# Modulation weights of layer 1 in half blocks, with two f32 tiles and one step per up iteration, in a two-layer diffusion block on Trainium2

## The chip, the cores and the metric

The kernel runs on one core of a Trainium2 chip. The metric is the device time of one execution in microseconds, here the median of three runs. Five engines work side by side and wait for each other by semaphores: TensorE (PE in the profile, its weight loads PEld), VectorE (DVE), ScalarE (ACT), GpSimd (POOL) and SyncE (SP), which issues the loads from HBM.

## The reference, cut to what matters

The reference is a model of two transformer-like layers with a conditioning vector, followed by a second block of four branches. The change touches the conditioning of layer 1 and runs during the feed-forward part (FFN) of layer 0. Shapes: 256 context tokens and 256 latent tokens, width 1024, FFN width 2816.

```python
D_MODEL = 1024
SEQ = 256
CTX_LEN = 256
D_FF = 2816

def modulate(x, g, shift, scale):
    return rmsnorm(x, g) * (1 + scale) + shift

def conv_ffn(h, w_up, conv_w, conv_b, w_down, rows):
    u = h @ w_up
    if rows is None:
        u = dwconv1d(u, conv_w[1], conv_b)
    else:
        u = dwconv2d_grid(u, conv_w, conv_b, rows)
    a, g = jnp.split(u, 2, axis=-1)
    return (jax.nn.silu(g) * a) @ w_down
```

In each layer six vectors of 1024 (shift, scale and gate for the mixer and for the FFN) are computed for the latent and for the context stream: a 1024-vector of the condition times a matrix `mod_w[layer]` of 1024 x 6144 in float32, plus `mod_b`. For layer 1 these are 24 MB of weights for two vectors, and they are needed when layer 1 begins (the first two), and later (the others).

## The kernel before

Weights come as float32 blocks of 1 MB. `get_w` (L318) loads a block into an f32 tile `st` by SyncE (`load_w`, L313), makes the high part `whi` in float16 on ScalarE (L324) and the low part `wlo` = `st` - `whi` in bfloat16 on VectorE or, with `eng=self.G`, on GpSimd (L325). The f32 tile is free again when the low part is done; the parts are free when TensorE has used them. Every product is three passes: high weights with high and low activations, low weights with high activations (`proj_fm`, L328).

`mod_steps` (L487) is a generator: one call of `next` runs one step. For one of the six vectors (`r`) it goes through four blocks `b` of 128 x 2048, that is two chunks of 128 rows by 1024 columns. A step loads and splits a block and multiplies it on TensorE: sixteen matmuls of 256 columns into one PSUM tile `mod`, four at a time in four column groups of the array. After the fourth block the row is copied out and turned into columns by small matmuls (L508).

`ffn(0, BOTH)` (L966) computes layer 0's FFN for all 512 tokens. *Up*: 22 iterations, each with one 1 MB block of `w_up`, split with GpSimd; two tiles of 24 matmuls with 512 columns; a 3x3 or 3-tap convolution on VectorE; the gating on ScalarE and GpSimd; the split of the result into `hid`. The first three iterations have their context half done ahead. *Down*: eight output tiles `k`, each from two half tiles of `w_dn` (128 x 1408, 704 KB), split with VectorE; 33 matmuls a half tile. For `k` = 0 to 5 a matmul has 512 columns. Tiles 6 and 7 are done for the context stream first (256 columns), then come its norm for layer 1, and then the same tiles for the latent stream. `layer1_mixer` begins with the products `dt` and `sx` on the normed context tokens.

The modulation steps of layer 1 are pulled in between: in up after every second iteration and after iteration 10 (twelve steps), in down after every half tile (twelve more). All their low parts are made on GpSimd. Their pools are `ms`, one f32 tile of 128 x 2048, and `mp`, two of each part.

The program is written in this order, and a planner with its own cost model orders the instructions on each engine before the run: at each point it takes the first instruction of the program that is ready by its costs. On the chip each engine, and SyncE's queue of loads, works through its list in that fixed order and waits where something is not there yet. With `start` and `stop` matmuls of one PSUM tile may stand apart, so the lists mix down and modulation matmuls.

Of the kernel before, what the change touches and what calls it, by code (L numbers as in the profile page):

```python
# [236 lines left out]
def bc(ap, axis, n):  # L237
    a = ap.unsqueeze(axis)
    shp = list(a.shape)
    shp[axis] = n  # L240
    return a.to_broadcast(shp)
# [7 lines left out]
class Program:  # L249
# [234 lines left out]
            self.stt(modA[:, 0, :, 2 * b:2 * b + 2], modc[:, r, :, 2 * b:2 * b + 2], 1.0, bc(g, 1, 2),  # L484
                     ALU.add, ALU.mult)

    def mod_steps(self, l, r, tag="mm", eng=None, pool=None, parts=None, whole=False):  # L487


        T, modc = self.T, self.modc[l]  # L490
        ps = self.ps(tag, "mod")
        for b in range(4):
            src = self.I["mod_w"][6 * l + r - 2, b]
            if whole:
                terms = [(self.cs, self.load_w(src, 2048, pool).rearrange("p (k n) -> p k n", k=2))]
            else:
                terms = [(self.c3, w) for w in self.get_w(src, 2, 1024, eng, pool, parts)]
            for k in range(2):
                for i, (c, w) in enumerate(terms):
                    for j in range(4):  # L500
                        T.matmul(ps[32 * j:32 * j + 32, :256], c[:, 2 * b + k], w[:, k, 256 * j:256 * j + 256],
                                 start=b == k == i == 0, stop=b == 3 and k == 1 and i == len(terms) - 1)
            if b < 3:
                yield
        row = self.cols.tile([128, 256], F32, tag="mrow", name="mrow", bufs=1)
        self.act(row, ps[:, :256])
        for c in range(2):
            T.matmul(ps[:, 256 + 8 * c:264 + 8 * c], row[:, c * 128:c * 128 + 128], self.msel8, start=True, stop=True)  # L508
        self.tt(modc[:, r].rearrange("p s (j c) -> p s j c", c=2), ps[:, 256:272].rearrange("p (c j s) -> p s j c", c=2, j=4),
                bc(self.modb[:, l, r].rearrange("p (j c) -> p j c", c=2), 1, 2), ALU.add)  # L510
        if r in (1, 4):
            self.stt(self.modA[l][:, r // 4], modc[:, r], 1.0, bc(self.ng[r // 4][:, l], 1, 2), ALU.add, ALU.mult)
        yield
# [452 lines left out]
    def ffn(self, l, streams):  # L966
        I, V = self.I, self.V
        both = len(streams) == 2
        n, t0 = (512, 0) if both else (256, 256)
        lat = n - 256  # L970
        fcb = self.pp("fcb").rearrange("p (l c) -> p l c", l=2)[:, l]
        h = self.h
        if both:

            self.norm_stream(l, 1, 1)
            first = []
            for i in range(3):
                w = self.get_w(I["w_up"][l, i], 8, 256, self.G)
                first.append((w, [self.mm("up") for _ in range(2)]))
                for c in range(2):  # L980
                    self.proj_fm(first[i][1][c][:, :256], w, c * 128, 128, h, 0, 256)
        else:
            self.norm_h(self.xT, t0, n, self.segs(l, 1, streams), h)

        def conv(u, ps, c):
            w = lambda j: fcw[:, c, j:j + 1]
            self.act(u[:, :n], ps[:, :n], AF.Identity, bias=fcb[:, c:c + 1], scale=w(4))
            if both:
                self.stt(u[:, 1:256], ps[:, 0:255], w(3), u[:, 1:256], ALU.mult, ALU.add)
                self.stt(u[:, 0:255], ps[:, 1:256], w(5), u[:, 0:255], ALU.mult, ALU.add)  # L990
            ug, pg = [a[:, lat:lat + 256].rearrange("p (r c) -> p r c", r=4) for a in (u, ps)]
            for dy in (-1, 0, 1):
                for dx in (-1, 0, 1):
                    if dy == 0 and dx == 0:
                        continue
                    r0, r1, c0, c1 = max(0, -dy), 4 - max(0, dy), max(0, -dx), 64 - max(0, dx)
                    o = ug[:, r0:r1, c0:c1]
                    self.stt(o, pg[:, r0 + dy:r1 + dy, c0 + dx:c1 + dx], w(3 * dy + dx + 4), o, ALU.mult, ALU.add)

        with ExitStack() as ph:  # L1000
            fp = self.pool("fp", 1, None, ph)
            f2 = self.pool("f2", 3, None, ph)
            stage = self.pool("stage", 1 if both else 3, None, ph)
            fcw = fp.tile([128, 44, 9], F32, name="fcw")
            self.nc.sync.dma_start(fcw, I["fcw"][l].rearrange("p (c j) -> p c j", c=44))
            hid = self.pair(fp, "hid", [128, 22, n])
            if both:
                ms, mp = self.pool("ms", 1, None, ph), self.pool("mp", 2, None, ph)
                mods = chain.from_iterable(self.mod_steps(1, r, eng=self.G, pool=ms, parts=mp) for r in range(6))
            for i in range(22):  # L1010
                begun = both and i < 3
                if begun:
                    w, pss = first[i]
                else:
                    w = self.get_w(I["w_up"][l, i], 8, 256, self.G, (None, stage)[i % 2])
                us = []
                for c in range(2):
                    ps = pss[c] if begun else self.mm("up")
                    a = 256 if begun else 0
                    self.proj_fm(ps[:, a:n], w, c * 128, 128, h, a, n)  # L1020
                    u = f2.tile([128, n], F32, tag=f"u{c}", name="u")
                    conv(u, ps, 22 * c + i)
                    us.append(u)
                sg = f2.tile([128, n], F32, tag="sg", name="sg")
                self.act(sg[:, :n], us[1][:, :n], AF.Silu)
                self.tt(sg[:, :n], sg[:, :n], us[0][:, :n], ALU.mult, eng=self.G)
                self.split(hid[0][:, i], hid[1][:, i], sg[:, :n], eng=self.G)
                if both and (i % 2 or i == 10):
                    next(mods)

            def down(k, ws, a, b):
                ps = self.mm("dn")
                for j, w in enumerate(ws):
                    self.proj_fm(ps[:, a:b], w, 0, 128, hid, a, b, nk=11, h0=11 * j, first=j == 0, last=j == 1)
                    if both:
                        next(mods, None)
                return ps

            def weights(k, j, parts=None):
                return self.get_w(I["w_dn"][l, 2 * k + j], 11, 128, self.G if not both and k < 2 else None, (None, stage)[j], parts)  # L1040

            if not both:
                self.ahead()
            for k in range(6 if both else 8):
                self.add_residual(down(k, [weights(k, j) for j in range(2)], 0, n), l, 5, k, streams, t0)
                if not both:
                    self.before_norm(k)
                    if k >= 4 and k < 4 + 3:
                        for i in (0, 1):
                            self.first_mg.append(self.get_w(I["w2_m"][2 * (k - 4) + i], 8, 128, self.G, stage, self.nx, 2048, 1024))  # L1050
            if both:

                ws = [[weights(k, j, fp if (k, j) == (7, 1) else None) for j in range(2)] for k in (6, 7)]
                for s, a, b in streams:
                    for k in (6, 7):
                        ps = down(k, ws[k - 6], a, b)
                        self.add_residual(ps[:, a:b], l, 5, k, ((s, 0, 256),), a)
                    if s == 0:
                        self.norm_stream(1, 0, 0)
# [878 lines left out]
```

## Time and profile before

| what | us |
|---|---|
| median of 3 runs (lowest, highest) | 1708.39 (1706.92, 1712.79) |
| the profiled execution, its time | 1712.42 |
| its span in the profile | 1710.6 |
| TensorE busy | 1601.9 (94%) |
| VectorE busy | 1198.7 (70%) |
| ScalarE busy | 845.7 (49%) |
| GpSimd busy | 538.7 (31%) |
| loads of `mod_w`, whole kernel | 40 of 1 MB |
| mean granted TensorE clock | 0.954 |

The profile is one execution. All times of the trace are counted from the start of the span; 1.8 us of the profiled execution lie around it. Busy shares are means over stages with different limits. A matmul's end is modelled, so a busy TensorE can also be one that waits between matmuls; the number of matmuls in a stretch tells more. Layer 0's FFN spans about 370 to 757 us: up until 610, down behind it.

### The profile page before, as it was taken

The page shows a single profiled execution, that of the slowest core. Times are in us where ns is not written, and L with a number is a line of the kernel's source. Part 1 is how long each engine was busy: PE and PEld are TensorE (multiplying, and loading weights), DVE is VectorE, ACT ScalarE, POOL GpSimd, SP SyncE. Part 2 cuts the span into 40 slices and gives each one's busy share as a digit, 9 for nine tenths or more (in the row PEclk, how much of TensorE's full clock was granted, in tenths as well). Part 3 has the DMA queues.
Part 4 walks back from the last instruction along what each step waited for, and adds up shares of the span by engine and source line. Part 5 has one row for each costly group of instructions (what it writes and reads, how often), then busy time and mean ns, then how long its engine had stood idle before and what let it go on. Part 6 is the DMA issues. An engine that isn't in the chain of part 4 may idle for free.

```text
span 1710.6 us, 31683 instructions
## 1 busy us (share of the span) xinstructions
PE 1601.9 (94%) x12978; PEld 1103.3 (64%) x12978; DVE 1198.7 (70%) x2600; ACT 845.7 (49%) x1366; POOL 538.7 (31%) x277
## 2 busy tenths in 40 slices
PE   6999999889999999898989898779999999999998
PEld 3566865476444444475566666568887787777877
DVE  5888745788778864457777676889976885455834
ACT  4746524445555443335554545356664644556442
POOL 0000000226887742311100000059954412332150
PEclk8999999899999999989989898989999989989999
DMA  9222127723443334432213222255455343333551
GB/s 380 95 86 75 52 86 260 298 102 127 145 172 133 128 139 172 153 121 88 86 50 123 73 100 80 76 195 198 153 183 201 112 161 124 118 142 105 222 173 50
DMA packets 37731, 236.78 MB, mean 138 GB/s; under 512 B 4304, under 2 KB 5072, under 8 KB 14672
## 3 DMA queue, kind: packets, MB, share of 16 engines
q1 hardware_dynamic: 37584, 234.74, 38.7%
q8 instruction: 102, 1.67, 0.4%
q14 instruction: 45, 0.37, 0.1%
HBM read 233.68 MB, written 1.05 MB: 137 GB/s over the span
## 4 chain that ended last, share of the span: by engine, by line
PE 74%; DVE 12%; ACT 4%; DMA 4%; issue 3%; POOL 2%; ACTq 0%; SPq 0%; DVEq 0%; POOLq 0%
PE up L332 19%; PE sx L332 5%; PE fm L332 4%; PE mg L332 4%; DVE wlo L294 3%; PE dn L332 3%; ACT whi L306 2%; PE sz L332 2%; PE br L332 2%; PE tm L339 2%; PE so L332 2%; DMA st<-in_mod_w_dram 2%; PE eo L332 2%; PE mqk L332 2%; PE sc L1601 2%
## 5 line engine op out<-in xcount | busy, mean ns | idle before, releaser
L294 POOL TENSOR_TENSOR wlo<-st,whi 128x2048 bf16<-128x2048 f32 (+2 forms) x114 | 408.1, 3584 | 923.7 <-ACT whi L306 873.6
L332 PEld LDWEIGHTS <-whi 128*128 128x128 f16 (+3 forms) x5240 | 517.3, 100 | 265.0 <-issue 40.6
L306 ACT ACTIVATE whi<-st 128x2048 f16<-128x2048 f32 (+3 forms) x218 | 365.5, 1685 | 318.4 <-DMA st<-in_mod_w_dram 59.1
L332 PEld LDWEIGHTS <-wlo 128*128 128x128 bf16 (+1 forms) x2620 | 261.2, 100 | 128.0 <-issue 11.8
L303 DVE SCALAR_TENSOR_TENSOR u<-up,fcw,u 128x189 f32<-128x189 f32 (+3 forms) x792 | 298.7, 433 | 47.9 <-ACT u L306 38.7
L294 DVE TENSOR_TENSOR wlo<-st,whi 128x2048 bf16<-128x2048 f32 (+3 forms) x104 | 242.0, 2330 | 108.5 <-ACT whi L306 107.3
L332 PE MATMUL up<-hh,whi 128*128 128x256 f16 (+1 forms) x752 | 239.4, 320 | 2.7 <-ACT hh L306 1.8
L332 PE MATMUL up<-hl,whi 128*128 128x256 bf16 (+1 forms) x752 | 239.1, 320 | 2.7 <-DVE hl L303 2.7
L332 PE MATMUL up<-hh,wlo 128*128 128x256 f16 (+1 forms) x752 | 238.6, 319 | 0.0
L332 PE MATMUL dn<-hidh,wlo 128*128 128x256 f16 (+1 forms) x396 | 124.0, 315 | 2.0 <-DVE wlo L294 2.0
L332 PE MATMUL dn<-hidh,whi 128*128 128x256 f16 (+1 forms) x396 | 124.0, 315 | 0.9 <-ACT whi L306 0.7
L332 PE MATMUL dn<-hidl,whi 128*128 128x256 bf16 (+1 forms) x396 | 124.2, 315 | 0.0
L332 PE MATMUL fm<-hh,whi 128*128 128x256 f16 x288 | 78.5, 273 | 0.5 <-DVE xc L303 0.5
L332 PE MATMUL fm<-hh,wlo 128*128 128x256 f16 x288 | 78.6, 273 | 0.0
L332 PE MATMUL fm<-hl,whi 128*128 128x256 bf16 x288 | 78.5, 273 | 0.0
L306 ACT ACTIVATE u<-up,ppt,fcw 128x512 f32<-128x512 f32 (+1 forms) x88 | 57.9, 659 | 37.9 <-PE up L332 37.7
L332 PE MATMUL mg<-hh,wlo 128*128 128x256 f16 x256 | 70.9, 277 | 3.6 <-POOL wlo L294 3.6
L298 POOL TENSOR_SCALAR E<-E,rs 128x128 f32<-128x128 f32 (+1 forms) x48 | 37.0, 785 | 114.7 <-DVE rs L1612 51.1
L332 PE MATMUL mg<-hl,whi 128*128 128x256 bf16 x256 | 71.0, 278 | 1.2 <-DVE hl L303 1.2
L332 PE MATMUL mg<-hh,whi 128*128 128x256 f16 x256 | 70.7, 277 | 0.9 <-ACT mgt L306 0.9
L339 PEld LDWEIGHTS <-hh 128*128 128x128 f16 x640 | 62.9, 101 | 9.9 <-issue 1.1
L332 PE MATMUL sx<-hl,whi 128*128 128x512 bf16 (+1 forms) x160 | 54.6, 342 | 0.0
(539 smaller groups left out, 3103.1 us busy)
## 6 DMA issues: line engine op xcount, KB each, us to landing
st<-in_w_up_dram SPq DMA_DIRECT2D x44, 1024.0 KB, 4.9
st<-in_mod_w_dram SPq DMA_DIRECT2D x40, 1024.0 KB, 5.0
st<-in_w_dram SPq DMA_DIRECT2D x25, 1024.0 KB, 4.9
st<-in_w_dn_dram SPq DMA_DIRECT2D x32, 704.0 KB, 4.1
st<-in_ssd_w_dram SPq DMA_DIRECT2D x20, 1024.0 KB, 4.8
st<-in_w_m_dram SPq DMA_DIRECT2D x32, 512.0 KB, 4.2
st<-in_even_w_dram SPq DMA_DIRECT2D x14, 1024.0 KB, 5.5
st<-in_mod_a_dram SPq DMA_DIRECT2D x8, 1024.0 KB, 16.8
```

The lines of the kernel that those rows point to most:

```text
L294: (eng or self.V).tensor_tensor(o, a, b, op=op)
L298: (eng or self.V).tensor_scalar(o, a, s1, None, op0=op0)
L303: self.V.scalar_tensor_tensor(o, a, s, b, op0=op0, op1=op1)
L306: self.S.activation(o, i, func, **kw)
L332: self.T.matmul(ps, w[a][:, k, c0:c0 + cw], h[b][:, h0 + k, t0:t1], start=first and k == 0 and i == 0, stop=last and k == nk - 1 and i == 2)
L339: self.T.matmul(ps, h[b][:, k, t0:t0 + 128], w[a][:, k, c0:c0 + cw], start=k == 0 and i == 0, stop=k == nk - 1 and i == 2)
L1601: T.matmul(ps[:, a:b], q[r, tb * 128:tb * 128 + 128], k[r, 0:b - a], start=True, stop=False)
```

## The change

`mod_steps` gets `halves`: a block is loaded as two halves of 128 x 1024 (512 KB), each with its own f32 tile and its own parts, and the generator yields after each half, so a vector takes eight steps and all six 48. `ms` has two f32 tiles of 128 x 1024 in place of one of 128 x 2048; `mp` has still two of each part, now half as large. In up one step follows every iteration (22 steps, eleven blocks' worth). In down three steps follow the first half tile of each output tile and two the second, until the remaining 26 are done. The engine of the low part is asked for when a step runs: GpSimd in up, VectorE in down (`up = False`). Other callers of `mod_steps` are as before.

```diff
--- before.py
+++ after.py
@@ -484,7 +484,8 @@
             self.stt(modA[:, 0, :, 2 * b:2 * b + 2], modc[:, r, :, 2 * b:2 * b + 2], 1.0, bc(g, 1, 2),
                      ALU.add, ALU.mult)
 
-    def mod_steps(self, l, r, tag="mm", eng=None, pool=None, parts=None, whole=False):
+    def mod_steps(self, l, r, tag="mm", eng=None, pool=None, parts=None, whole=False, halves=False):
+
 
 
         T, modc = self.T, self.modc[l]
@@ -493,13 +494,18 @@
             src = self.I["mod_w"][6 * l + r - 2, b]
             if whole:
                 terms = [(self.cs, self.load_w(src, 2048, pool).rearrange("p (k n) -> p k n", k=2))]
-            else:
+            elif not halves:
                 terms = [(self.c3, w) for w in self.get_w(src, 2, 1024, eng, pool, parts)]
             for k in range(2):
+                if halves:
+                    both = self.get_w(src[:, 1024 * k:1024 * k + 1024], 1, 1024, eng(), pool, parts, 1024)
+                    terms = [(self.c3, w) for w in both]
                 for i, (c, w) in enumerate(terms):
                     for j in range(4):
-                        T.matmul(ps[32 * j:32 * j + 32, :256], c[:, 2 * b + k], w[:, k, 256 * j:256 * j + 256],
+                        T.matmul(ps[32 * j:32 * j + 32, :256], c[:, 2 * b + k], w[:, 0 if halves else k, 256 * j:256 * j + 256],
                                  start=b == k == i == 0, stop=b == 3 and k == 1 and i == len(terms) - 1)
+                if halves and k == 0:
+                    yield
             if b < 3:
                 yield
         row = self.cols.tile([128, 256], F32, tag="mrow", name="mrow", bufs=1)
@@ -1005,8 +1011,10 @@
             self.nc.sync.dma_start(fcw, I["fcw"][l].rearrange("p (c j) -> p c j", c=44))
             hid = self.pair(fp, "hid", [128, 22, n])
             if both:
-                ms, mp = self.pool("ms", 1, None, ph), self.pool("mp", 2, None, ph)
-                mods = chain.from_iterable(self.mod_steps(1, r, eng=self.G, pool=ms, parts=mp) for r in range(6))
+                ms, mp = self.pool("ms", 2, None, ph), self.pool("mp", 2, None, ph)
+                up = True
+                mods = chain.from_iterable(self.mod_steps(1, r, eng=lambda: self.G if up else None, pool=ms, parts=mp,
+                                                          halves=True) for r in range(6))
             for i in range(22):
                 begun = both and i < 3
                 if begun:
@@ -1025,20 +1033,21 @@
                 self.act(sg[:, :n], us[1][:, :n], AF.Silu)
                 self.tt(sg[:, :n], sg[:, :n], us[0][:, :n], ALU.mult, eng=self.G)
                 self.split(hid[0][:, i], hid[1][:, i], sg[:, :n], eng=self.G)
-                if both and (i % 2 or i == 10):
+                if both:
                     next(mods)
 
             def down(k, ws, a, b):
                 ps = self.mm("dn")
                 for j, w in enumerate(ws):
                     self.proj_fm(ps[:, a:b], w, 0, 128, hid, a, b, nk=11, h0=11 * j, first=j == 0, last=j == 1)
-                    if both:
+                    for _ in range(3 - j if both else 0):
                         next(mods, None)
                 return ps
 
             def weights(k, j, parts=None):
                 return self.get_w(I["w_dn"][l, 2 * k + j], 11, 128, self.G if not both and k < 2 else None, (None, stage)[j], parts)
 
+            up = False
             if not both:
                 self.ahead()
             for k in range(6 if both else 8):
```

## Rows read from the trace of the kernel before

**Rows 1.** Windows, layer 0's FFN and layer 1's start: length; busy us of each engine; clock; DMA

```profile
core 0: us, PE busy (x) PEld busy (x) DVE busy (x) ACT busy (x) POOL busy (x), PEclk, DMA share, GB/s
...
399.00:610.00 211.00, 211.00 (x1161) 98.34 (x1162) 171.66 (x420) 111.21 (x116) 168.15 (x71) 1.00 0.44 151
...
654.00:737.00 83.00, 72.77 (x465) 38.28 (x465) 33.61 (x26) 25.61 (x21) 24.57 (x7) 0.94 0.46 161
...
787.00:830.00 43.00, 36.23 (x247) 24.59 (x245) 40.18 (x65) 28.22 (x39) 8.16 (x2) 0.92 0.43 144
...
610.40:757.20 146.80, 132.67 (x878) 71.58 (x874) 71.19 (x83) 53.61 (x55) 49.76 (x15) 0.96 0.43 152
```

**Rows 2.** Chain that ended last, up: start us, us, what

```profile
491.66 0.55 PE mod L501 x16
...
492.21 10.47 PE up L332 x48
...
502.68 0.55 PE mod L501 x16
```

**Rows 3.** Chain that ended last, down

```profile
641.97 6.05 DMA st<-in_mod_w_dram
...
648.10 1.92 ACT whi L306
...
650.09 4.09 POOL wlo L294
```

**Rows 4.** Timeline, GpSimd, down

```profile
613.66 4.07 POOL L294 TENSOR_TENSOR wlo<-st,whi 128x2048 bf16<-128x2048 f32 x1 [2.73 <-ACT whi L306]
...
689.18 4.06 POOL L294 TENSOR_TENSOR wlo<-st,whi 128x2048 bf16<-128x2048 f32 x1 [11.65 <-ACT whi L306]
...
737.11 4.07 POOL L294 TENSOR_TENSOR wlo<-st,whi 128x2048 bf16<-128x2048 f32 x1 [7.32 <-ACT whi L306]
```

**Rows 5.** Waits, 610 to 757 us: us in total, times, longest

```profile
ACT whi L306 <- DMA st<-in_mod_w_dram: 53.5, 9, 8.5
```

**Rows 6.** Timeline, TensorE, first and last down matmul, layer 1's first

```profile
610.40 0.39 PE L332 MATMUL dn<-hidh,whi 128*128 128x512 f16 x1
...
754.12 0.27 PE L332 MATMUL dn<-hidh,wlo 128*128 128x256 f16 x1
...
757.24 0.42 PE L332 MATMUL dt<-hh,whi 128*64 128x256 f16 x1 [2.85 <-DVE xT L303]
```

**Rows 7.** DMA issues in down, in up, and at 1300 to 1500 us

```profile
st<-in_mod_w_dram SPq DMA_DIRECT2D x10, 1024.0 KB, 5.1
...
st<-in_mod_w_dram SPq DMA_DIRECT2D x11, 1024.0 KB, 4.9
...
st<-in_w_m_dram SPq DMA_DIRECT2D x13, 512.0 KB, 4.2
```

**Rows 8.** Instructions on 1024 columns: ScalarE after 1100 us; GpSimd, ns min/median/max

```profile
L306 ACT ACTIVATE whi<-st 128x1024 f16<-128x1024 f32 x32 | 33.6, 1052 | 31.6 <-DMA st<-in_w_m_dram 19.6 <-PE mg L332 10.8 <-issue 1.1
...
L294 POOL TENSOR_TENSOR wlo<-st,whi x114: 2121/4074/4251, 332.2 to 1668.3; 128x2048 bf16<-128x2048 f32 x78, 128x1024 bf16<-128x1024 f32 x32, 128x1408 bf16<-128x1408 f32 x4
```

**Rows 9.** Timeline, VectorE, down

```profile
690.40 4.32 DVE L294 TENSOR_TENSOR wlo<-st,whi 128x1408 bf16<-128x1408 f32 x1 [8.74 <-ACT whi L306]
...
722.31 3.16 DVE L294 TENSOR_TENSOR wlo<-st,whi 128x1408 bf16<-128x1408 f32 x2 [4.74 <-ACT whi L306]
...
736.93 0.48 DVE L303 SCALAR_TENSOR_TENSOR xT<-dn,modc,xT 128x256 f32<-128x256 f32 x1 [6.48 <-PE dn L332]
...
737.96 3.50 DVE L294 TENSOR_TENSOR sq<-sq,s 128x256 f32<-128x256 f32 x1 [0.54 <-ACT s L306]
...
742.46 0.69 DVE L294 TENSOR_TENSOR wlo<-st,whi 128x512 bf16<-128x512 f32 x1
...
747.20 0.42 DVE L294 TENSOR_TENSOR sq<-sq,s 128x256 f32<-128x256 f32 x1
```

**Rows 10.** Groups by form, 610 to 757 us: busy us, mean ns | idle before

```profile
L294 DVE TENSOR_TENSOR wlo<-st,whi 128x1408 bf16<-128x1408 f32 x14 | 41.2, 2948 | 41.2 <-ACT whi L306 41.2
```

## The prediction

> **What bounds the kernel now.** I read the stretches first. From 399 to 610 us TensorE is busy throughout at a granted clock of 1.00 (2.4 GHz); from 654 to 737 us the mean clock falls to 0.94 and TensorE's busy time to 72.8 of 83 us, with no other engine near full [rows 1]. So the up half of layer 0's FFN is bound by TensorE and the down half by something else. The chain of waits tells what. In up it is matmuls end to end: 10.47 us for the 48 of an iteration, 0.55 us for a modulation block [rows 2]. In down it is load, ScalarE, GpSimd, load again: 6.05 + 1.92 + 4.09 us for a 1 MB modulation block [rows 3], because the next load waits until the one f32 tile is split. GpSimd's queue gives the period: the first of its eleven modulation splits in down begins at 613.66 us, the last at 737.11, so 123.45 / 10 = 12.3 us a block [rows 4].
>
> TensorE executes in a fixed order in which the modulation matmuls stand between the down matmuls. A block that comes late holds the down matmuls behind it; on ScalarE the wait for the modulation load, 53.5 us in nine waits [rows 5], stands ahead of the down weights' own splits. The size of the loss: from the first down matmul at 610.40 us to the end of the last at 754.12 + 0.27 [rows 6] are 144.0 us. The work is six output tiles of 66 matmuls each, 512 columns, at 10.47 / 48 = 0.218 us, 396 x 0.218 = 86.3; the last two tiles, 264 matmuls of 256 columns at half that, 28.8; twelve blocks at 0.55, 6.6; and some 3 for the small matmuls of rows and norms: 124.7. TensorE loses 19.3 us here.
>
> **The change, part by part.**
>
> *Halves with two f32 tiles.* A block becomes two halves of 512 KB, and one half loads while the other is split. The cycle of one f32 tile is load, ScalarE split, low split. Loads of 512 KB elsewhere in the trace land in 4.2 us, those of 1 MB here in 5.1 (median) [rows 7]; ScalarE takes 1.05 us for 1024 columns [rows 8]. VectorE's low split of 1024 columns is not in the trace: 512 take 0.69 us and 1408 take 3.16 / 2 = 1.58 [rows 9], so 1.2 by the line between them. With some 0.15 us of hand-over the cycle is 4.2 + 1.05 + 1.2 + 0.15 = 6.6 us; two tiles give a half every 3.3 us, a block every 6.6 where it was 12.3. TensorE's demand: two half tiles of down are 66 x 0.218 = 14.4 us, five steps 5 x 0.275 = 1.4, so 15.8 us for five halves, 3.15 us a half. The loads then lag by 0.15 us a half, 4 us over 26 halves. From below the lag is nothing, since steps in bursts of three and two leave loads time to land. From above: 1 MB loads in down took up to 6.05 us on the chain [rows 3] against 4.9 in up [rows 7]; 1.2 us more a load makes 3.9 us a half, 26 x 0.75 = 19 us of lag. I take 5 us, near the lower end, because the DMA engines are busy only 43 to 46% of down [rows 1], and the 512 KB rows are the nearest.
>
> The Trainium skill (DMA: Bandwidth & Descriptors, section Bandwidth) speaks against smaller transfers: it asks for 1 MiB or more in each. The fit on the same page (section Anatomy of one DMA; taken there on GpSimd's queue), 2.0 us and 436 GB/s, gives as an estimate 3.2 us for 512 KB and 4.4 for 1 MB, so two halves would cost 6.4 us of load where a block costs 4.4; with two tiles in flight a half would still come every 2.8 us, there would be no lag, and the sum below would be 5 us better. The trace differs from the fit: 4.2 us for 512 KB [rows 7].
>
> *VectorE splits in down.* A down-weight split on VectorE that begins inside one of GpSimd's 4.06 us splits lasts 4.32 us instead of 1.58: it begins at 690.40 and ends at 694.72, which is 1.48 us after GpSimd's end at 693.24, as if it had started there [rows 4, 9]. Even a sum of squares of 0.42 us lasts 3.50 beside GpSimd [rows 9]. The fourteen splits of down take 41.2 us [rows 10], of which 14 x 1.58 = 22 are work. With GpSimd's splits gone from down, VectorE gains 26 x 1.2 = 31 us of work and loses 19 us of blocked time; it was busy 71 of 147 us [rows 1], so this has room. One of the delays lies on the chain that ends the stage: the last residual of the context half begins at 736.93 us, its sum of squares is blocked for 3.1 us, the norm follows, and TensorE takes up layer 1 at 757.24, 2.85 us after its last down matmul [rows 6, 9]. Without the block this chain of 20.3 us is 17.2.
>
> *Steps moved.* Up has 22 halves, eleven blocks' worth, instead of twelve blocks: 0.55 us of TensorE moves to down, nothing in sum. GpSimd is busy 168 of 211 us in up [rows 1], about 8.5 us an iteration of 10.7; a half of 2.12 us [rows 8] each iteration in place of a whole of 4.1 in about every second leaves that as it is. SyncE issues two loads an iteration in up, seven in 15.8 us in down. ScalarE splits 26 x 1.05 = 27.3 us of modulation in down instead of 12 x 1.92 = 23, with 93 us idle there [rows 1]. All this is hidden under matmuls; if up's cover is gone, see the second rival.
>
> *The sum.* With no lag the context half of down would end at 610.4 - 0.55 + 86.3 + 14.4 (its 132 matmuls of 256 columns) + 26 x 0.275 + 2 = 719.7 us; with 5 us at 724.7. The last residual stood at 736.93, so 12.2 us are won. The chain behind gives 3.1 more. Layer 1 starts at about 724.7 + 17.2 = 742 instead of 757.2, **15.3 us earlier**. What follows is paced by TensorE and by this start: layer 1's first weights are split as the down weights come free. So I let the whole gain stand. The profiled execution's 1712.4 us becomes 1697.1. That execution stands 4.0 us above the median of 1708.4, so the median goes to **1693**.
>
> **The rivals.** *The loads still set the pace* (lag 19 us): the context half ends 14 us later than in the sum, and of 15.3 us some 2 to 6 remain: 1702 to 1706. For it: loads of 6 us beside those of down weights. Against it: the DMA engines are half idle. A smaller version: the third step after a half tile finds only two part tiles; if its matmuls stand directly behind, TensorE waits for ScalarE and VectorE, 1.05 + 1.2 less 0.55, in each of five tiles, 8.5 us in place of the lag of 5: 1697.
>
> *GpSimd binds up* (the slower one). A step after every iteration makes every iteration wait for a low split. GpSimd's 8.5 us leave 2.2 us for its own waits for ScalarE; from waits of 2.2 + 15.3 / 22 = 2.9 us an iteration the gain is gone, and at 3.6 us the run is 15 us slower in net: 1723. Against it: where three iterations in a row carry a whole block each, GpSimd has some 10.6 us of work in each, and TensorE ran them at 10.47 + 0.55 [rows 2]. For it: 80% of GpSimd's time in up is used.
>
> *The gain is lost behind.* Layer 1's first blocks go through a VectorE stretch, 40.2 of 43 us busy [rows 1]. If a load came late there behind the extra issues on SyncE, or another order on the engines cost as much, the median would stay at 1704 to 1712; this is also where the change would do what it says and nothing come of it.
>
> **How the numbers follow.** The forecast (gain 7 to 23 us) 0.66; loads still set the pace 0.14; lost behind 0.11; GpSimd binds up 0.09. About 0.3%, 5.1 us, is what a measurement here can tell from no change. Faster: 0.66 and most of 0.14, 0.78; same: 0.13; slower: 0.09. The low end is no lag and no gap: 19.3 + 3.1 + 1, so 1685. The high end, 1708, takes in the lagging loads and half of the case lost behind. The likeliest case alone spans 1685 to 1701.
>
> **What would show it.** Right: a granted clock of 1.00 through down; from the first down matmul to the last some 130 us instead of 144; no GpSimd split in down after the last gating; VectorE's 1408-column splits at 1.6 us; layer 1's first matmul near 742 us; up still 10.7 to 11 us an iteration. Wrong: a wait for the modulation load that still heads ScalarE's list in down; 512 KB loads above 5.4 us; up iterations above 11 us; or layer 1 starting early and the kernel ending no earlier.

## The result, and the profile after

The changed kernel takes 1691.14 us (median of 4 runs, 1687.17 to 1696.52) where the kernel before takes 1710.59 (4 runs, 1706.92 to 1713.95): ratio 0.9889, 95% interval 0.9851 to 0.9927. It was timed twice more beside the kernel before, with ratios of 0.992 (0.9895 to 0.9944) and 0.9928 (0.9904 to 0.9951). So it is faster by 0.5 to 1.5%. The forecast of 1693 lies 2 us off, but several of its terms were wrong, in opposite directions.

The profiled execution took 1687.17 us, its span is 1685.0. First the same kind of stretches as in [rows 1], moved with the work:

```profile
core 0: us, PE busy (x) PEld busy (x) DVE busy (x) ACT busy (x) POOL busy (x), PEclk, DMA share, GB/s
399.00:610.00 211.00, 210.00 (x1105) 94.98 (x1123) 168.86 (x416) 109.71 (x125) 165.00 (x79) 1.00 0.43 148
609.80:742.10 132.30, 130.98 (x883) 68.91 (x891) 75.90 (x99) 57.32 (x66) 5.96 (x4) 1.00 0.55 178
654.00:727.00 73.00, 72.08 (x475) 37.02 (x480) 36.77 (x42) 27.44 (x29) 0.00 (x0) 1.00 0.54 177
770.00:813.00 43.00, 34.45 (x242) 23.88 (x243) 38.97 (x63) 27.19 (x36) 8.15 (x2) 0.96 0.36 124
```

The second line is the whole difference at layer 1's start: from the first down matmul to layer 1's first are 132.3 us where they were 146.8. TensorE, busy in 90% of that stretch before, is busy in 99%, at a granted clock of 1.00 (2.4 GHz) instead of 0.96. GpSimd has 6 us left there, of the gating. Up is as it was.

TensorE's own waits over the stretch say the same. Before, they sum to 14.0 us, and these are the two largest entries:

```profile
PE mod L501 <- ACT whi L306: 8.9, 4, 4.0
PE dt L332 <- DVE xT L303: 2.8, 1, 2.8
```

After, they sum to 0.7 us:

```profile
PE mod L505 <- DVE wlo L294: 0.4, 1, 0.4
PE dn L332 <- issue: 0.3, 2, 0.2
```

A smaller part of the loss before was the clock. Behind a wait of 4.05 us that ends at 689 us, the down matmuls of the kernel before start 0.43 us apart instead of 0.22, at a granted clock of 0.50 (1.2 GHz):

```profile
689.00:695.00 6.00, 5.85 (x17) 2.05 (x17) 4.32 (x1) 1.37 (x2) 4.06 (x1) 0.50 0.13 19
```

The timeline of VectorE shows the two ends of the tail, which in [rows 9] are 736.93 and 737.96:

```profile
726.98 0.48 DVE L303 SCALAR_TENSOR_TENSOR xT<-dn,modc,xT 128x256 f32<-128x256 f32 x1 [5.75 <-PE dn L332]
728.01 0.43 DVE L294 TENSOR_TENSOR sq<-sq,s 128x256 f32<-128x256 f32 x1 [0.54 <-ACT s L306]
```

The last context residual, at 736.93 before, begins at 726.98, and the sum of squares behind it lasts 0.43 us instead of 3.50. The groups by form, 610 to 742 us, on VectorE (busy us, mean ns, idle before), answer to [rows 10]:

```profile
L294 DVE TENSOR_TENSOR wlo<-st,whi 128x1024 bf16<-128x1024 f32 x25 | 30.5, 1223 | 27.0 <-ACT whi L306 27.0
L294 DVE TENSOR_TENSOR wlo<-st,whi 128x1408 bf16<-128x1408 f32 x14 | 22.7, 1624 | 6.5 <-ACT whi L306 6.3
```

The down splits fall from 2948 to 1624 ns each. The issues of loads in down [rows 7] and the heaviest wait there [rows 5]:

```profile
st<-in_mod_w_dram SPq DMA_DIRECT2D x23, 512.0 KB, 4.7
```

```profile
ACT whi L306 <- DMA st<-in_mod_w_dram: 36.5, 18, 4.1
```

Half the bytes land in 4.7 us where the whole landed in 5.1, and ScalarE still waits for these loads more than for anything else. Last, the chain of work in down, which was load, ScalarE, GpSimd [rows 3], in its longer pieces:

```profile
630.86 5.81 DMA st<-in_mod_w_dram
636.78 1.06 ACT whi L306
637.87 1.24 DVE wlo L294
639.12 5.26 DMA st<-in_mod_w_dram
644.48 2.33 ACT whi L306 x2
647.28 1.10 issue
648.38 0.42 DVE sq L294
648.80 1.14 DVE wlo L294
649.96 5.13 DMA st<-in_mod_w_dram
```

It is still a chain of loads and splits, from 621 to 696 us; only then does it pass to the down matmuls. But it ends in a wait of TensorE of 0.4 us. In the second profile of the changed kernel (e2_after_again) TensorE waits for nothing from the first down matmul to layer 1's first, and the chain of that stretch is almost wholly TensorE's own matmuls. First the window of its context part (defined below), then its chain from 608.2 to 742 us:

```profile
608.20:724.87 116.67, 116.67 (x758) 55.55 (x755) 65.55 (x76) 49.62 (x54) 6.00 (x4) 1.00 0.56 186
```

```profile
by line: PE dn L332 85.9%; PE mod L505 8.0%; issue 1.7%; ACT whi L306 1.4%; PE mod L514 1.3%; PE dt L332 0.5%; PE rbc L375 0.3%; DVE sq L294 0.3%; DVE hl L303 0.3%; PE ssq L367 0.3%; DVE wlo L294 0.0%
```

So the loads no longer set the pace of down; TensorE does.

### The profile page after: what moved, and what is told of

It reads as the page before. It is cut to its first block, busy times and chain, and to the rows that moved or that the text cites. A ratio compares the mean times of both kernels' runs of the same rounds, so it can differ in the third digit from the quotient of the medians.

```text
span 1685.0 us, 31758 instructions
## 1 busy us (share of the span) xinstructions
PE 1582.5 (94%) x12915; PEld 1087.5 (65%) x12978; DVE 1203.0 (71%) x2626; ACT 848.8 (50%) x1390; POOL 488.5 (29%) x275
## 4 chain that ended last, share of the span: by engine, by line
PE 74%; DVE 12%; ACT 4%; DMA 4%; issue 3%; POOL 1%; ACTq 0%; SPq 0%; DVEq 0%; POOLq 0%
PE up L332 18%; PE dn L332 5%; PE sx L332 5%; PE fm L332 4%; PE mg L332 3%; DVE wlo L294 3%; ACT whi L306 3%; PE sz L332 2%; PE br L332 2%; DMA st<-in_mod_w_dram 2%; PE so L332 2%; PE eo L332 2%; PE mqk L332 2%; PE tm L339 2%; PE sc L1610 1%
## 5 line engine op out<-in xcount | busy, mean ns | idle before, releaser
L332 PEld LDWEIGHTS <-whi 128*128 128x128 f16 (+2 forms) x5240 | 512.5, 99 | 257.9 <-issue 38.8
L294 POOL TENSOR_TENSOR wlo<-st,whi 128x1024 bf16<-128x1024 f32 (+2 forms) x112 | 354.8, 3177 | 943.2 <-ACT whi L306 599.5
L306 ACT ACTIVATE whi<-st 128x2048 f16<-128x2048 f32 (+3 forms) x242 | 369.5, 1537 | 266.9 <-PE up L332 40.5
L332 PEld LDWEIGHTS <-wlo 128*128 128x128 bf16 (+2 forms) x2620 | 259.5, 99 | 129.4 <-issue 12.3
L294 DVE TENSOR_TENSOR wlo<-st,whi 128x2048 bf16<-128x2048 f32 (+3 forms) x130 | 253.4, 1954 | 98.5 <-ACT whi L306 97.0
L332 PE MATMUL up<-hl,whi 128*128 128x256 bf16 (+1 forms) x733 | 231.1, 317 | 2.7 <-DVE hl L303 2.7
L332 PE MATMUL dn<-hidl,whi 128*128 128x256 bf16 (+1 forms) x384 | 117.3, 306 | 0.0
L332 PE MATMUL sx<-hh,wlo 128*128 128x512 f16 (+1 forms) x160 | 53.3, 336 | 0.5
```

Source lines behind the costliest of these rows:

```text
L294: (eng or self.V).tensor_tensor(o, a, b, op=op)
L306: self.S.activation(o, i, func, **kw)
L332: self.T.matmul(ps, w[a][:, k, c0:c0 + cw], h[b][:, h0 + k, t0:t1], start=first and k == 0 and i == 0, stop=last and k == nk - 1 and i == 2)
```

## The experiments

The change does two things in down: it shortens the cycle in which an f32 tile is loaded, split and loaded again, and it takes GpSimd off VectorE's way. **Theory 1:** the cycle was what TensorE lost; halves and two tiles gave it back. **Theory 2:** moving the split to VectorE was enough, by a faster split, by VectorE's own splits and sums running unblocked, or both; halves and tiles brought nothing. **Theory 3:** each has its share. The table gives every run. "Context part" is from the first down matmul to the last context residual, "tail" from there to layer 1's first matmul, both in the profiled execution; the kernel before had 126.5 and 20.3 there, the first run of the changed kernel 117.2 and 15.1. In e7_whole_twice 33 matmuls of the latent stream, 3.6 us, stand ahead of the last context residual that stand behind it elsewhere, so its sum, 140.8, is what compares.

| run | us, median (range, runs) | ratio to before, 95% | context part + tail, us |
|---|---|---|---|
| e1_before_again | 1705.67 (1696.75 to 1709.34, 10) | 1.002, 0.9997 to 1.0042 | 127.3 + 20.0 |
| e2_after_again | 1689.18 (1687.13 to 1691.42, 4) | 0.992, 0.9895 to 0.9944 | 116.7 + 15.1 |
| e3_halves_gpsimd | 1700.83 (1692.68 to 1712.48, 10) | 0.9982, 0.9956 to 1.0008 | 123.4 + 15.1 |
| e4_whole_vector | 1686.82 (1686.41 to 1687.35, 4) | 0.9906, 0.9883 to 0.9928 | 114.3 + 15.1 |
| e5_one_half_tile | 1745.17 (1741.1 to 1747.67, 4) | 1.0236, 1.0193 to 1.0278 | 180.8 in all |
| e6_halves_beside | 1696.05 (1692.17 to 1699.62, 10) | 0.994, 0.9912 to 0.9967 | 123.9 + 15.1 |
| e7_whole_twice | 1701.44 (1698.65 to 1712.26, 10) | 1.0, 0.9971 to 1.0028 | 126.8 + 14.0 |
| e8_three_tiles | 1691.34 (1685.34 to 1698.88, 6) | 0.9931, 0.9892 to 0.997 | 114.8 + 15.1 |
| e9_all_in_up | 1692.11 (1684.32 to 1700.0, 10) | 0.9946, 0.9923 to 0.9969 | 102.4 + 15.1 |
| e10_whole_vector_2 | 1688.05 (1684.09 to 1696.89, 11) | 0.9937, 0.9916 to 0.9958 | 113.5 + 15.1 |
| e11_after_3 | 1687.9 (1685.23 to 1694.3, 6) | 0.9928, 0.9904 to 0.9951 | 116.7 + 15.1 |

**The two kernels once more** (no edit).

> The kernel before, profiled a second time. Layer 1's first matmul is expected at 757 us again, plus or minus 1. The profile after is 25.6 us shorter than the one before, of which 15.1 us were won by layer 1's start and 8 us in the second block's stretch. If those 8 us are scatter between executions, this profile's stretch from the first to the last fm matmul lies anywhere from 246 to 255 us; if they belong to the kernel before, it is 254 us again.

> The changed kernel, profiled a second time. Layer 1's first matmul at 742 us, plus or minus 1. If the 8 us of the second block are scatter, the stretch from the first to the last fm matmul is between 246 and 255 us; if they belong to the change, 247 us again.

Both repeat within a few tenths of a per cent. Layer 1 begins at 757.0 us, as expected, and at 740.0, 2 us sooner than in the first profile, where 1 was allowed.

**Halves without the move of the engine**, the changed kernel with every modulation split on GpSimd:

```diff
-  eng=lambda: self.G if up else None, pool=ms, parts=mp,
+  eng=lambda: self.G, pool=ms, parts=mp,
```

> The changed kernel, but GpSimd splits the low parts in down as well. Theory (both the load cycle and VectorE's blocked splits cost): the cycle of one f32 tile is 4.7 + 1.05 + 2.12 + 0.15 = 8.0 us, a half every 4.0 us against the 3.15 that TensorE asks for, and VectorE's 1408-column splits are blocked again for up to 2.1 us each: layer 1's first matmul at 747 to 755 us, time 1697 to 1705. Rival 1 (two f32 tiles alone bring the gain): 742 to 744 us, 1693 or less. Rival 2 (the engine alone brings it): 755 to 757 us, 1705 to 1710.

Layer 1 begins at 749.0 us, about half way between the two kernels; in the time of the whole kernel no gain shows, since the interval of its ratio holds 1. The context part gains 3 to 4 us; the tail gains all of its 5, since the last GpSimd split in down begins at 708.97 us and no longer lies over the context norm. VectorE's down splits still take 2041 ns on average.

**The move of the engine without halves**, the kernel before (1 MB blocks, one f32 tile, the old steps) with VectorE in down:

```diff
-  mods = chain.from_iterable(self.mod_steps(1, r, eng=self.G, pool=ms, parts=mp) for r in range(6))
+  up = True
+  mods = chain.from_iterable(self.mod_steps(1, r, eng=lambda: self.G if up else None, pool=ms, parts=mp) for r in range(6))
...
+  up = False    # ahead of down; get_w is given eng()
```

> The kernel before, but VectorE splits the low parts in down: whole 1 MB blocks, one f32 tile, steps where they were. Theory: the cycle is 5.6 + 1.92 + 2.28 + 0.15 = 10 us a block, where it was 12.3 and where TensorE asks for one in 7.7; VectorE is no longer blocked: layer 1's first matmul at 746 to 752 us, time 1698 to 1704. Rival 1 (two tiles alone): 755 to 757 us, 1705 to 1710. Rival 2 (engine alone): 742 to 744 us, 1691 to 1694.

This alone brings the whole gain, as Theory 2 has it. Layer 1 begins at 739.1 us, sooner than the numbers I gave and than in the changed kernel. The groups by form of VectorE, and SyncE's queue with three of the block loads in a row:

```profile
L294 DVE TENSOR_TENSOR wlo<-st,whi 128x2048 bf16<-128x2048 f32 x13 | 29.8, 2290 | 35.9 <-ACT whi L306 35.9
L294 DVE TENSOR_TENSOR wlo<-st,whi 128x1408 bf16<-128x1408 f32 x14 | 22.6, 1618 | 2.1 <-ACT whi L306 2.0
```

```profile
643.44 0.33 SPq L315 DMA_DIRECT2D st<-in_mod_w_dram  x1
652.43 0.33 SPq L315 DMA_DIRECT2D st<-in_mod_w_dram  x1
661.86 0.33 SPq L315 DMA_DIRECT2D st<-in_mod_w_dram  x1
```

A block takes 2.29 us on VectorE where GpSimd took 4.07 [rows 4], and the loads follow at 9.0 and 9.4 us where the period was 12.3; over its eleven splits in down, 613.18 to 706.09 us, the period is 92.91 / 10 = 9.3. TensorE's list puts 33 down matmuls, 7.2 us, and a block of 0.55 in turn: 7.8. So one tile is still 1.5 us a block too slow, and little comes of it. TensorE multiplies thirteen blocks from 609 us on, and SyncE issues ten loads: three blocks were loaded when down began. The first is used at once, the other two are worth 2 x 7.8 = 15.6 us, against 12 x 1.5 = 18 for the twelve that follow. That leaves 2.4 us of lag. TensorE's list of waits in the context part has 2.3 us for VectorE's splits of blocks, and 1.0 for other things; the prediction's terms without lag, 86.3 + 14.4 + 6.6 + 2 = 109.3, are 5.0 us less than 114.3, so 1.7 us are no wait at all. My number for this run was too high because it had no head start.

**What the second tile is for**, the changed kernel with one f32 tile of half size:

```diff
-  ms, mp = self.pool("ms", 2, None, ph), self.pool("mp", 2, None, ph)
+  ms, mp = self.pool("ms", 1, None, ph), self.pool("mp", 2, None, ph)
```

> The changed kernel with one f32 half tile in place of two; VectorE splits in down. Theory C (the load cycle of the f32 tile sets the pace): a half every 4.7 + 1.05 + 1.22 + 0.15 = 7.1 us where TensorE asks for one in 3.15; even if the planner foresees most of it, layer 1's first matmul comes after 752 us, time above 1698. Theory B (what cost was GpSimd's splits, which hold VectorE up, and only that): 740 to 745 us, 1687 to 1692.

As C has it, and far past its 752 us: layer 1 begins at 792.5, and the kernel is slower than before by 2.4%. Its chain is the bare cycle of one tile:

```profile
690.83 3.47 DMA st<-in_mod_w_dram
...
694.38 1.07 ACT whi L306
...
695.46 1.24 DVE wlo L294
...
696.72 3.61 DMA st<-in_mod_w_dram
```

```profile
660.00:735.00 75.00, 36.56 (x203) 14.65 (x202) 22.35 (x24) 18.02 (x19) 0.00 (x0) 0.68 0.34 109
```

A half comes every 6 us, 12 a block. The windows line shows TensorE busy half of the time at a clock of 0.68. In SyncE's queue five modulation loads stand from 665.04 to 691.15 us and seven from 702.75 to 739.49, each waiting for the tile, and the down weights' loads behind them wait too. The second tile is needed because the blocks were halved; it is no gain by itself.

**GpSimd beside VectorE**, the changed kernel, in which GpSimd in down reads each finished low part and writes a tile that nobody uses:

```diff
+  if eng() is None:
+      beside = self.beside.tile([128, 1024], BF16, tag="beside", name="beside")
+      self.tt(beside, both[1][:, 0], both[1][:, 0], ALU.subtract, eng=self.G)
```

> The changed kernel with an idle instruction more: in down GpSimd reads each half's low part (128 x 1024) and writes the difference, zero, to a tile that nobody reads. It stands behind VectorE's split, so that the f32 tile's own cycle is as in the changed kernel, but GpSimd reads SBUF for 26 x 2.1 us beside VectorE. Theory B (blocking): layer 1's first matmul at 745 to 750 us, near the 749 of halves split by GpSimd. Theory C (load cycle): 740 to 743 us as in the changed kernel, unless the next half's split is itself blocked, by at most 2.1 us of a 7.1 us cycle.

B holds, at its lower edge: layer 1 begins at 745.4 us. Loads (4.7 us), tiles and steps are those of the changed kernel, only GpSimd is busy beside (610 to 740 us):

```profile
L294 DVE TENSOR_TENSOR wlo<-st,whi 128x1024 bf16<-128x1024 f32 x25 | 37.4, 1509 | 20.3 <-ACT whi L306 20.2
L294 DVE TENSOR_TENSOR wlo<-st,whi 128x1408 bf16<-128x1408 f32 x13 | 27.1, 2086 | 1.4 <-ACT whi L306 1.4
L294 POOL TENSOR_TENSOR beside<-wlo 128x1024 bf16<-128x1024 bf16 x25 | 63.3, 2534 | 28.7 <-DVE wlo L294 25.0 <-DVE modA L303 3.4
```

VectorE's splits grow from 1223 to 1509 and from 1624 to 2086 ns, and the context part from 117 to 123.9 us; TensorE waits 5.6 us in it, all for VectorE's splits, and no wait for a low part's tile, which GpSimd now holds longer, stands in the lists. So blocking alone, with a short cycle, costs some 7 us there. As down begins at 606.4 us in this profile, 2 to 3 us sooner, layer 1 begins 3 to 6 us later than in the changed kernel, and the two don't differ measurably in the time of the whole kernel (0.994 beside 0.992 and 0.9928). The Trainium skill (SBUF — State Buffer, section Who interferes with whom) says that a VectorE instruction with two inputs in SBUF contends with a GpSimd instruction that reads SBUF; these rows agree, with 1509 ns against 1223.

**The long cycle without GpSimd**, e4_whole_vector with the low part made twice, one after the other, in down:

```diff
-        self.tt(lo[:, :n], st[:, :n], hi[:, :n], ALU.subtract, eng=eng)
+        for _ in range(2 if twice else 1):
+            self.tt(lo[:, :n], st[:, :n], hi[:, :n], ALU.subtract, eng=eng)
```

> Whole 1 MB blocks with one f32 tile and VectorE in down, but each modulation block's low part is computed twice in a row there (the second time the same numbers). The cycle is 4.8 + 1.92 + 4.58 + 0.2 = 11.5 us a block, nearly the 12.3 of before, with no GpSimd beside VectorE. Theory C: nearly the loss of before, layer 1's first matmul at 750 to 756 us. Theory B: 739 to 744 us.

Near C, 1 us short of it: layer 1 begins at 749.4 us. The loads follow at about 12 us (666.58, 678.85, 690.30 us in SyncE's queue), as before, while the down splits take 1659 ns as after. The whole stretch takes 140.8 us, 11 more than in e4_whole_vector and 6 less than before. The second split also occupies VectorE, but the chain from 617 to 731 us is load, ScalarE, two splits, load again, so it is the cycle that is felt. In the time of the whole kernel no gain shows (1.0).

**A third f32 tile** (`self.pool("ms", 3, None, ph)`):

> The changed kernel with three f32 half tiles. A half every 2.4 us, faster than the 3.15 that TensorE asks for. If loads still cost the changed kernel anything, layer 1's first matmul comes at 737 to 739 us instead of 740 to 742 and the time falls by 2 to 3 us; if the head start of two split and two loaded halves already covers the lag, nothing moves by more than 1 us.

The context part is 2 us shorter, the median no different that can be measured. Loads have no part in the 2 us: TensorE waited for none with two tiles in e2_after_again either.

**Two steps in every up iteration** (`for _ in range(2 if both else 0)` in place of `if both`), so that only four halves are left for down:

> The changed kernel with two half steps in each up iteration in place of one: 44 of the 48 halves in up, all but four with their low parts on GpSimd, and only four left for down. GpSimd then has 2.44 + 4.07 us of an iteration's own work and 2 x 2.12 us of low parts, 10.75 us, against TensorE's 10.47 + 0.55 = 11.02. Theory A (TensorE still sets the pace of up): up takes 22 x 0.275 = 6 us longer and down as much less; with hardly any modulation loads in down there is no lag, so layer 1 starts at 736 to 742 us and the median equals the changed kernel's within 5 us. Theory B (GpSimd, which also waits for ScalarE in each iteration, binds): an iteration takes 1 us or more longer than 11.0, the first down matmul comes at 638 us or later in place of 616, layer 1 starts after 758 and the median is 1705 or more.

Mostly A. Windows and groups by form, 430 to 600 us, in which GpSimd has 47 low parts to make:

```profile
430.00:600.00 170.00, 170.00 (x965) 72.32 (x963) 127.64 (x302) 96.85 (x109) 162.85 (x78) 1.00 0.55 184
```

```profile
L294 POOL TENSOR_TENSOR wlo<-st,whi 128x1024 bf16<-128x1024 f32 x32 | 68.6, 2154 | 1.2 <-ACT whi L306 1.2
```

GpSimd is busy 96% of the time and TensorE loses nothing to it: from 399 to 623 us TensorE has no wait and is busy throughout. The first down matmul comes at 623.1 us, 13 to 15 us later than in the changed kernel, more than the 6 expected. The moved matmuls account for it: 44 groups of four, at some 0.31 us each among other matmuls (next section), are 13.6 us. Down gives all of it back, and layer 1 begins at 740.6.

**The engine alone, once more, beside the changed kernel:**

> The kernel before with VectorE making the low parts in down, once more, with more rounds and beside the changed kernel, as the version that may be best. Theory D (the engine alone brings the gain): median 1685 to 1690, within 0.3% of the changed kernel in the same batch; from the first down matmul to layer 1's first 129 to 131 us. Rival (its lead over the changed kernel in the first batch was real): 2 to 6 us faster than the changed kernel, with an interval that leaves out no difference.

> The changed kernel once more, as the one to compare with: median 1687 to 1692, from the first down matmul to layer 1's first 131 to 133 us.

D holds: 1688.05 and 1687.9 us. The 2 us by which layer 1 begins sooner in e10_whole_vector_2 (737.7 and 739.8) don't show in the medians; from the first down matmul to layer 1's first are 128.6 us, just under the 129 expected. No version tried beats the changed kernel measurably.

## Why the prediction was right, point by point

**What bound the kernel.** Right. With a cycle as long as before and no GpSimd beside VectorE (e7_whole_twice) the stretch from down's first matmul to layer 1's first takes 140.8 us, with a shorter cycle (e4_whole_vector) 129.4: the cycle costs 11 of the 17 us that are won there. My model of the down matmuls is confirmed by e9_all_in_up, whose four halves in down make 86.3 + 14.4 + 1.1 + 2 = 103.8 us by the prediction's terms; 102.4 were measured. With so few modulation matmuls it does not test their price.

**The lag and the price of a half: the step that was off.** I took a cycle of 6.6 us, so a half every 3.3 us and 5 us of lag. VectorE's first 1024-column split in down begins at 612.67 us, the last of 25 at 702.42: 89.75 / 24 = 3.74 us. The price of VectorE's split was right (1.22 us). The load was not: 4.7 median and 5.1 to 5.8 on the chain instead of 4.2, and on the chain a half also queues behind a down weight's split on ScalarE (2.33 us for the two) and for VectorE (0.5 to 1.4 us); turns of 8.3 and 10.8 us stand in the lines above. With 3.74 my formula, 26 x (3.74 - 3.15), would have given 15.3 us of lag. (For the upper bound I took 6.05 us as the longest load on the chain of before; one of 7.65 stands there too, at 679.45.) The context part is indeed 7.3 us longer than the 109.9 of the sum (719.7 - 609.85). But that is no lag: TensorE waits 0.7 us there in the first profile and nothing in e2_after_again and e11_after_3, with 116.7 us in both.

It is TensorE's own work, in a term that I took from sixteen modulation matmuls in a row [rows 2], 0.275 us for a half's eight. In down they stand in groups of four among the down matmuls (e2_after_again):

```profile
628.77 0.38 PE L332 MATMUL dn<-hidh,whi 128*128 128x512 f16 x1
629.08 0.29 PE L505 MATMUL mod<-whi,c 128*32 128x256 f16 x4
629.30 0.39 PE L332 MATMUL dn<-hidl,whi 128*128 128x512 bf16 x1
629.53 0.38 PE L332 MATMUL dn<-hidh,wlo 128*128 128x512 f16 x1
629.84 0.29 PE L505 MATMUL mod<-wlo,c 128*32 128x256 bf16 x4
630.07 0.39 PE L332 MATMUL dn<-hidh,whi 128*128 128x512 f16 x1
```

Around a group two down matmuls are 0.53 us apart (628.77 and 629.30) instead of 0.22, so a lone group costs 0.31 us and a half in two groups 0.62. The first step, from the down matmul to the group, is 0.30 to 0.32 us at all 38 places of the context part, and in up of e9_all_in_up, where TensorE never waits, as well; so it is not a hidden wait for loads. Of the 116.7 us, 86.3 and 14.4 are down matmuls. The other 16.0 went to 26 halves and the small matmuls of four finished rows, where I had 26 x 0.275 + 2 = 9.15. The whole blocks of e4_whole_vector leave 114.3 - 100.7 - 3.3 of waits = 10.3 us. With a half at (16.0 - 2) / 26 = 0.54 us, TensorE asks for one every (14.4 + 5 x 0.54) / 5 = 3.4 us, and the lag by my formula is 26 x (3.74 - 3.4) = 8.8. A head start that I left out covers that: TensorE multiplies 27 halves from 609 us on and SyncE issues 23 loads, so four were loaded when down began; the first is used at once, and three are worth 3 x 3.4 = 10.2 us. So 5 us of lag that did not come stand against some 7 us of matmuls that did.

The Trainium skill (DMA: Bandwidth & Descriptors, section Bandwidth) asks for large transfers, and the landing times agree: half the bytes took 4.7 us where the whole took 5.1. That this halving did no harm is the second tile's doing (e5_one_half_tile).

**The tail: mis-sized the other way.** I priced GpSimd over the context norm at 3.1 us, a tail of 17.2. It is 15.1, a gain of 5.2, because TensorE now sets its length: it is busy in all 15.10 us, mostly with the latent stream's matmuls, and the norm is done under them. Before, it waited 0.8 us for the sum of squares and 2.8 for VectorE's last steps ahead of layer 1, and sixteen modulation matmuls with their row took 1.0 us more; the other 0.5 us stay open. A part of this gain is only moved. Layer 1's second matmul now waits for the norm, which it did not before (757.46 us):

```profile
743.50 0.27 PE L332 MATMUL dt<-hl,whi 128*64 128x256 bf16 x1 [1.12 <-DVE hl L303]
```

By this matmul 14.0 us are won, by the first 15.1. So 10.0 us in the context part instead of 12.2, and 5.2 instead of 3.1 in the tail: the sum, 15.1, and layer 1 at 742.08 us are as forecast, by errors that cancel. That is luck.

**VectorE's blocked time.** The row was read rightly, but the prediction saw a cost only in the tail. The chain of the kernel before has three such splits, each 4.34 us instead of 1.6. Twice a modulation load follows behind it, since SyncE's queue holds the down weight's load that waits for the split's tile ahead of the modulation load:

```profile
637.18 4.34 DVE wlo L294
...
641.54 0.33 SPq L315
...
641.97 6.05 DMA st<-in_mod_w_dram
...
674.67 4.34 DVE wlo L294
...
679.03 0.33 SPq L315
...
679.45 7.65 DMA st<-in_mod_w_dram
```

And e6_halves_beside shows that it costs some 7 us in the context part even when the cycle is short. The gains don't add: halves alone bring about 8 us from down's first matmul to layer 1's first (e3_halves_gpsimd), the engine alone 17, both together 15. With the engine moved, 3.3 us of waits were left for the halves to win, and their groups of four cost TensorE 16.0 us where whole blocks cost 10.3.

**Steps moved.** Up stayed as it was, and the rival *GpSimd binds up* was far off: with twice its modulation splits in up TensorE still waited for nothing there (e9_all_in_up).

**The gain stands.** By the median it does: 19.5 us in the first comparison, 14 and 13 in the later ones (1703.44 and 1700.91 for before), against 15 to 17 at layer 1's first matmul and 14 to 16 at its second. In the two first profiles the spans differ by 25.6 us, 10 more than at layer 1's start. Those I don't put down to the change: the final matrix products of the second block last 254.6 and 251.6 us in two executions of before, 246.9, 248.5 and 251.6 in three of the changed kernel, 251.6 and 245.2 in two of e4_whole_vector's kernel. One kernel's own executions differ by 3 to 6 us there; what sets it stayed open.

**What I missed.** No rival said that the engine alone would do. I had the row for it: 4.09 of the 12.3 us were GpSimd's, and VectorE's rate was known. With 2.3 us in its place the cycle is 10.5 (9.3 came), and VectorE's own work unblocks with it. I costed the parts of the change in one sum and never each by itself. One sign that I named as "wrong" was none: the wait for the modulation load still heads ScalarE's list, but ScalarE has time to spare, and TensorE, which has none, waited 0.7 us at most.

## What to carry to other kernels

When a change has several parts, work out what each would bring by itself: here moving one split to another engine gave the whole gain, and the halves, the second tile and the finer steps nothing more. A lag is (cycle - demand) times the count, less what is ready when the stage begins: 18 less 15.6 us for the blocks of e4_whole_vector, where 2.3 were waited. Take the demand from matmuls as they will stand in the list: a half was priced at 0.275 us and took 0.54. And when a chain passes through loads, look at the waits of the engine that bounds the stage before calling the loads the limit. Halving a transfer is no gain where its landing time hardly falls, and with a single buffer the landing is paid twice for the same bytes.

## What the runs showed of the hardware that was not expected

Beside other loads, 512 KB landed in 4.5 to 4.7 us in three profiles of the changed kernel and 1 MB in 4.8 to 5.1 with whole blocks (medians in down); in e5_one_half_tile, where one load at a time was under way for most of the stretch, 512 KB took 3.5 us on the chain. GpSimd reading SBUF beside VectorE's two-input subtractions lengthened them by 23 to 28% on average (1223 to 1509 and 1624 to 2086 ns). Four modulation matmuls of 256 columns, alone between down matmuls of 512, cost TensorE 0.31 us (0.53 less 0.22); sixteen in a row took 0.55. GpSimd could be kept busy 96% of a stretch that it did not bind.
